# A diffusion block on one core: the residual's scaling moved in VectorE's queue, the decays' sums made float32r

## The chip, the cores and the metric

One core of a Trainium2 chip runs the whole program. The metric is the device time of an execution in microseconds (us). The engines are TensorE (PE, its weight loads PEld), VectorE (DVE), ScalarE (ACT), GpSimd (POOL) and SyncE (SP, which issues most of the DMAs).

## The reference

Two layers of a diffusion block work on 512 tokens x and 256 context tokens, 1024 wide, in float32. Each layer is a gated feed-forward, a mixer of four kinds of attention, and a second feed-forward; each is followed by a layer norm of the scaled residual plus the branch.

```python
def post_norm(x, f, g, b):
    return layer_norm(ALPHA * x + f, g, b)

def swiglu(h, w_in, w_out):
    a, u = jnp.split(h @ w_in, 2, axis=-1)
    return (jax.nn.silu(a) * u) @ w_out

def ssd_chunked(x, dt, A, Bh, Ch, h0):
    ...
    cum = jnp.cumsum(dtc * A, axis=2)
    seg = cum[:, :, :, None, :] - cum[:, :, None, :, :]
    lmat = jnp.exp(jnp.where(tril, seg, -jnp.inf))
    att = jnp.einsum('bcihn,bcjhn->bcijh', Cc, Bc) * lmat * dtc[:, :, None]
    ...
    y = y + jnp.einsum('bcihn,bchpn,bcih->bcihp', Cc, jnp.moveaxis(h_start, 0, 1), jnp.exp(cum))
```

One of the four parts of the mixer is this state-space part (SSD): in chunks of 128 tokens, 4 heads, in two directions. `seg` are sums of `dt * A` over the tokens between two, `cum` sums up to one; the second layer leaves out the context's outputs.

## The kernel before

The code is written as straight program text, and a scheduler puts each instruction into the queue of its engine; each engine works its queue in order. Some places call `tc.issue_after(ins)`: what is written inside it is queued behind `ins` on the engine of `ins`.

**Products.** A float32 matrix is split into a high part (float32r, by ACT, L328) and the rest (by DVE, L329), and a product is three float32r matmuls (`mm3`, L335 to L337).

**Feed-forward (`ffn`).** The 22 column blocks f of the hidden width are done in parts: (0,4), (4,8), ... with the context, and (0,6), (6,12), ... in the last feed-forward. In the first part, f = 0 and 1 are plain products (`first`), while DVE and POOL make sums for the others (`sums`: L573 to L576, split at L565, L566). The others are `winograd`: seven products of 12 matmuls each. In the order of the code they are B11, B21, T2, B22, T3, T4 and T1. DVE adds them up at L689 to L703; L692 reads T2 and must be done before T3 is written, since both lie in one PSUM tile, and L693 stands likewise between B22 and T4. In the last feed-forward, even f are `eight` (plain). `store` then splits the gated g (ACT L646, DVE L647). `branch_out` multiplies a part with the second weights and adds it to the residual `res` (L472, L474).

**The residual.** `res` must be scaled by ALPHA (and the norm's gain and shift, `rescale`, L465: 2 x 12 DVE operations with the context, 2 x 8 without) before the first part is added to it. This was written behind the first part as `self.behind`, and the scheduler was free to queue it earlier. For the first feed-forward it is `scale_input` (L359, 6 operations). `merge`, behind the mixer, does it too.

**SSD.** `ssd` runs beside the projections of the other attention kinds (`side_by_side`), so that their `mm3` stand between its steps in PE's queue. `chunk_out(t)` is called for 6 chunks in layer 0 (two of them in one direction) and 4 in layer 1. POOL makes `ld` = dtA times a triangle (L1294, two operations), PE sums it against another triangle (L1299, 8 float32 matmuls, which the trace holds as 16), ACT takes the exponential (L1301), DVE makes `att` (L1310 to L1313), and PE multiplies (L1319). PE also makes the decays `two` from dtA (L1330, 8 float32 matmuls, 16 in the trace; half in a one-direction chunk) and the states' part (L1332).

## Time and profile before

| what | us |
|---|---|
| median of 3 runs | 2965.39 (2965.01 to 2967.98) |
| the profiled execution | 2970.67 |
| its span | 2968.9 |

The profile is of one execution. A stretch of the span is given as start and end in us from the span's start. The feed-forwards' first parts lie at 48 to 98 (first, layer 0), 1085 to 1150 (second, layer 0), 1660 to 1730 (first, layer 1) and 2590 to 2632 (second, layer 1); the SSD chunks at 712 to 800 and 2305 to 2362. Idle time of PE is a stretch's length less its busy time; the granted clock is a share of 2.4 GHz, and a mean over the stretch of the two levels 2.4 and 1.2 GHz.

### The profile page before, as it was taken

The page shows a single profiled execution, that of the slowest core. Times are in us where ns is not written, and L with a number is a line of the kernel's source. Part 1 is how long each engine was busy: PE and PEld are TensorE (multiplying, and loading weights), DVE is VectorE, ACT ScalarE, POOL GpSimd, SP SyncE. Part 2 cuts the span into 40 slices and gives each one's busy share as a digit, 9 for nine tenths or more (in the row PEclk, how much of TensorE's full clock was granted, in tenths as well). Part 3 has the DMA queues.
Part 4 walks back from the last instruction along what each step waited for, and adds up shares of the span by engine and source line. Part 5 has one row for each costly group of instructions (what it writes and reads, how often), then busy time and mean ns, then how long its engine had stood idle before and what let it go on. Part 6 is the DMA issues. An engine that isn't in the chain of part 4 may idle for free.

```text
span 2968.9 us, 43652 instructions
## 1 busy us (share of the span) xinstructions
PE 2867.3 (97%) x16412; PEld 2451.8 (83%) x16412; DVE 2068.6 (70%) x4258; ACT 1149.6 (39%) x2103; POOL 494.2 (17%) x372
## 2 busy tenths in 40 slices
PE   7999999999999998999999999999999999899997
PEld 4898888888787777888878789999988787788886
DVE  4766668775758787666577976766886757776558
ACT  4333233352256543322324433333344256443333
POOL 1222122100110002221211122221200110012112
PEclk9999999999999999999999999999999999999998
DMA  6443334231124223534435122212132143242332
GB/s 230 144 162 107 121 100 141 77 100 49 29 78 83 94 72 104 178 122 141 157 103 168 57 67 75 76 58 74 56 97 72 44 110 89 78 125 86 95 100 72
DMA packets 319207, 296.09 MB, mean 100 GB/s; under 512 B 16311, under 2 KB 244751, under 8 KB 318739
## 3 DMA queue, kind: packets, MB, share of 16 engines
q1 hardware_dynamic: 317939, 290.80, 31.6%
q0 software_dynamic: 1056, 2.49, 0.4%
q8 instruction: 130, 2.13, 0.3%
q14 instruction: 82, 0.67, 0.1%
HBM read 270.52 MB, written 7.39 MB: 94 GB/s over the span
## 4 chain that ended last, share of the span: by engine, by line
PE 77%; DVE 15%; issue 3%; ACT 2%; DMA 2%; POOL 0%; SPq 0%; DVEq 0%; ACTq 0%; POOLq 0%
PE ps L335 12%; PE ps L337 12%; PE ps L336 12%; PE psp L335 9%; PE psp L337 9%; PE psp L336 9%; PE ps L260 2%; PE ps L1033 2%; DVE wl L329 2%; PE ps L1075 2%; DVE tmp L472 2%; PE psp L1091 2%; DVE res L465 2%; DVE res L474 1%; DVE actl L392 1%
## 5 line engine op out<-in xcount | busy, mean ns | idle before, releaser
L328 ACT CAST wh<-wraw 128x512 fp32r<-128x512 f32 x570 | 352.1, 621 | 873.2 <-PE ps L337 457.2
L329 DVE TENSOR_TENSOR wl<-wraw,wh 128x512 fp32r<-128x512 f32 x570 | 416.0, 736 | 330.4 <-ACT wh L328 324.2
L335 PE MATMUL psp<-acth,wh 128*128 128x384 f32 (+2 forms) x1432 | 482.9, 338 | 4.5 <-DVE e L701 1.9
L336 PE MATMUL psp<-actl,wh 128*128 128x384 f32 (+2 forms) x1432 | 481.0, 336 | 5.1 <-DVE actl L392 4.9
L337 PE MATMUL psp<-acth,wl 128*128 128x384 f32 (+2 forms) x1432 | 478.6, 335 | 4.6 <-DVE wl L329 4.6
L335 PEld LDWEIGHTS psp<-acth,wh 128*128 128x128 f32 x1432 | 271.6, 190 | 44.7 <-issue 27.3
L328 ACT CAST wh<-wrax 128x512 fp32r<-128x512 f32 x280 | 173.9, 622 | 339.9 <-PE ps L336 201.6
L336 PEld LDWEIGHTS psp<-actl,wh 128*128 128x128 f32 x1432 | 271.9, 190 | 20.3 <-DVE actl L392 7.0
L337 PEld LDWEIGHTS psp<-acth,wl 128*128 128x128 f32 x1432 | 272.2, 190 | 16.2 <-DVE wl L329 5.2
L335 PE MATMUL ps<-S,wh 128*128 128x384 f32 (+1 forms) x840 | 276.7, 329 | 7.8 <-DVE e L692 4.8
L336 PE MATMUL ps<-S,wh 128*128 128x384 f32 (+1 forms) x840 | 275.8, 328 | 0.0
L337 PE MATMUL ps<-S,wl 128*128 128x384 f32 (+1 forms) x840 | 275.6, 328 | 0.0
L329 DVE TENSOR_TENSOR wl<-wrax,wh 128x512 fp32r<-128x512 f32 x280 | 212.5, 764 | 84.3 <-ACT wh L328 59.0
L335 PE MATMUL ps<-acth,wh 128*128 128x512 f32 (+2 forms) x688 | 245.7, 358 | 3.2 <-ACT wh L328 1.7
L336 PE MATMUL ps<-actl,wh 128*128 128x512 f32 (+2 forms) x688 | 244.2, 355 | 0.0
L337 PE MATMUL ps<-acth,wl 128*128 128x512 f32 (+2 forms) x688 | 243.3, 354 | 0.0
L335 PE MATMUL ps<-wh,gTh 128*128 128x512 f32 x594 | 235.1, 396 | 7.6 <-DVE tmp L472 7.6
L337 PE MATMUL ps<-wh,gTl 128*128 128x512 f32 x594 | 233.4, 393 | 0.0
L336 PE MATMUL ps<-wl,gTh 128*128 128x512 f32 x594 | 233.4, 393 | 0.0
L474 DVE TENSOR_TENSOR res<-res,tmp 128x512 f32<-128x512 f32 x268 | 188.0, 732 | 0.6
L335 PEld LDWEIGHTS ps<-S,wh 128*128 128x128 f32 x840 | 159.2, 189 | 12.6 <-issue 6.8
L337 PEld LDWEIGHTS ps<-S,wl 128*128 128x128 f32 x840 | 159.3, 190 | 0.0
(376 smaller groups left out, 5470.8 us busy)
## 6 DMA issues: line engine op xcount, KB each, us to landing
araw<-in_ada_w_dram SPq DMA_DIRECT2D x128, 512.0 KB
wraw<-in_ffn_w_out_dram SPq DMA_DIRECT2D x88, 512.0 KB
wrax<-in_ffn_w_in_dram SPq DMA_DIRECT2D x160, 256.0 KB
wraw<-in_ffn_w_in_dram SPq DMA_DIRECT2D x120, 256.0 KB
wraw<-in_mix_w_in_dram SPq DMA_DIRECT2D x44, 512.0 KB
wraw<-in_ffn_w_in_dram SPq DMA_DIRECT2D x36, 512.0 KB
wraw<-in_mix_w_out_dram SPq DMA_DIRECT2D x16, 512.0 KB
mrow<-mrow SPq DMA_DIRECT2D x10, 512.0 KB
```

The costliest lines, as they stand in the source:

```text
L260: nc.tensor.matmul(ps[32 * g:32 * g + 32, :], lhsT=self.cs[:, k, c0:c0 + 32], rhs=w[:, k - kk, :], start=i == 0 and k < 4, stop=i == len(n ...
L328: self.nc.scalar.copy(h, raw)
L329: self.nc.vector.tensor_tensor(lo, raw, h.bitcast(F32), op=ALU.subtract)
L335: mm(out, lhsT=a[0], rhs=b[0], start=start, stop=False)
L336: mm(out, lhsT=a[0], rhs=b[1], start=False, stop=False)
L337: return mm(out, lhsT=a[1], rhs=b[0], start=False, stop=stop)
L465: nc.vector.tensor_tensor(r, r, x[:, lo:hi], op=op)
L472: nc.vector.tensor_tensor(y, acc, mrow[0 if t < 4 else 1][:, dh * 512:(dh + 1) * 512], op=ALU.mult)
L474: nc.vector.tensor_tensor(r, r, y, op=ALU.add)
L1033: nc.tensor.matmul(ps[:, at:at + hi - lo], lhsT=q, rhs=part[:, lo:hi], start=i == 0, stop=i == 1)
L1075: nc.tensor.transpose(pt[:, j * P:(j + 1) * P], p[:, a:a + P], self.ident)
L1091: nc.tensor.matmul(out[64 * a:64 * a + 64, :], lhsT=v[:, kt, vcol:vcol + 64], rhs=pT[:, i], start=i == 0, stop=i == len(order) - 1)
```

## The change

Two things. First, `rescale` and `scale_input` get a step, and `ffn` calls them at the last two f of the first part: one half is queued behind the store of the last but one f, the other behind that of the last. The loads and ACT's work on the gain come before the step and are not bound. Second, in `ssd`, dtA is split into two float32r parts. `ld` becomes four tiles: the high parts by POOL, the low ones by ACT (8 operations a chunk), as products with U and L. PE sums them with GT and LT as weights, in 4 matmuls of 512 columns for all heads. `two` is made from the same `ld` tiles, with two weights `half` that hold ones in 64 columns, in 8 matmuls of 256 columns. So `ld`, which has one buffer, is now read until `two` is done.

```diff
--- before.py
+++ after.py
@@ -355,6 +355,7 @@
             self.nc.sync.dma_start(self.res[i], src)
 
     def scale_input(self, pool, tiles):
+        yield
         for r in self.res:
             self.nc.vector.tensor_scalar(r, r, ALPHA, None, op0=ALU.mult)
             yield
@@ -458,6 +459,7 @@
         gb = self.gain(l, i, self.side or tmp, tags)
         for x in gb:
             nc.scalar.mul(x, x, ALPHA)
+        yield
         for lo, hi in ((0, 512), (512, D)):
             for t in tiles:
                 for x, op in zip(gb, (ALU.mult, ALU.add)):
@@ -644,7 +646,7 @@
         def store(g, f, lo):
             gh, gl = gT[0][:, f - lo], gT[1][:, f - lo]
             nc.scalar.copy(gh, g)
-            nc.vector.tensor_tensor(gl, g, gh.bitcast(F32), op=ALU.subtract)
+            return nc.vector.tensor_tensor(gl, g, gh.bitcast(F32), op=ALU.subtract)
 
         def first(late):
 
@@ -722,10 +724,17 @@
                     winograd(f, g, todo[1:])
                 else:
                     eight(f, g)
-                store(g, f, lo)
+                end = store(g, f, lo)
+                if lo == 0 and f >= hi - 2:
+                    if f == hi - 2:
+                        behind = self.behind(pool, tiles)
+                        next(behind)
+                    with self.tc.issue_after(end.ins):
+                        next(behind)
             if lo == 0:
-                for _ in self.behind(pool, tiles):
-                    pass
+                with self.tc.issue_after(end.ins):
+                    for _ in behind:
+                        pass
             if mrow is None:
                 mrow = self.mod_rows(l, which, pool, (0, 1) if with_ctx else (0,))
             a_of = lambda f, t: tuple(g[:, f - lo, t * P:(t + 1) * P] for g in gT)
@@ -1218,6 +1227,18 @@
         self.softplus(dtf, tmp)
         dtA = self.sb(tmp, [6, 8], "dtA")
         nc.vector.tensor_tensor(dtA, dt, bcast1(self.A[:, l], 6), op=ALU.mult)
+
+        parts = [self.sb(tmp, [6, 8], x, F32R) for x in ("dtAh", "dtAl")]
+        nc.scalar.copy(parts[0], dtA)
+        nc.vector.tensor_tensor(parts[1], dtA, parts[0].bitcast(F32), op=ALU.subtract)
+        before = [self.sb(tmp, [P], x, F32R) for x in ("GTr", "LTr")]
+        for x, m in zip(before, (GT, LT)):
+            nc.scalar.copy(x, m)
+
+        halves = [self.sb(tmp, [P], f"half{a}", F32R) for a in range(2)]
+        for a, x in enumerate(halves):
+            nc.vector.tensor_copy(x, self.zero.to_broadcast([P, P]))
+            nc.vector.tensor_copy(x[:, 64 * a:64 * a + 64], self.ones[:, :64])
         ps = self.ps1()
         for d, m in ((0, GT), (1, LT)):
             nc.tensor.matmul(ps[:, 24 * d:24 * d + 24].rearrange("p (t e) -> p t e", t=6), lhsT=m,
@@ -1288,15 +1309,18 @@
             q = col(t)
             first = {4: (1,), 5: (0,)}.get(t, (0, 1))
 
+            seg = self.ps1()
             ld = []
-            for d, m in ((0, GT), (1, LT)):
-                x = self.sb(tmp, [4, P], f"ld{d}", bufs=1)
-                nc.gpsimd.tensor_tensor(x, bcast(dtA[:, t, 4 * d:4 * d + 4], P), bcast1(m, 4), op=ALU.mult)
-                ld.append(x)
-            seg = self.ps1()
-            for h in range(4):
-                for d, m in ((0, U), (1, L)):
-                    nc.tensor.matmul(seg[:, h * P:(h + 1) * P], lhsT=ld[d][:, h], rhs=m, start=d == 0, stop=d == 1)
+            for d, m in ((0, U), (1, L)):
+                hi, lo = (self.sb(tmp, [4, P], f"ld{d}{i}", F32R, bufs=1) for i in range(2))
+                ld.append((hi, lo))
+                nc.gpsimd.tensor_tensor(hi, bcast(parts[0][:, t, 4 * d:4 * d + 4].bitcast(F32), P), bcast1(m, 4),
+                                        op=ALU.mult)
+                for h in range(4):
+                    nc.scalar.mul(lo[:, h], m, parts[1][:, t, 4 * d + h:4 * d + h + 1].bitcast(F32))
+                for i, x in enumerate((hi, lo)):
+                    nc.tensor.matmul(seg, lhsT=before[d], rhs=x.rearrange("p h c -> p (h c)"), start=d + i == 0,
+                                     stop=d + i == 2)
             E = self.sb(tmp, [2, 2, P], "segE", bufs=1)
             nc.scalar.activation(E.rearrange("p g r c -> p (g r c)"), seg, AF.Exp)
             G = self.ps1()
@@ -1320,15 +1344,14 @@
                                          rhs=att[d][:, pr, a], start=d == 0, stop=d == 1)
 
             two = self.ps2()
-            for d, m in ((0, U), (1, L)):
-                if d not in first:
-                    continue
+            for d in first:
+                for i in range(4):
+                    x = ld[d][i // 2].rearrange("p (r a) c -> p a r c", a=2)[:, i % 2]
+                    nc.tensor.matmul(two[:, 0, 256 * d:256 * d + 256].rearrange("p (r c) -> p r c", r=2), lhsT=halves[i % 2],
+                                     rhs=x, start=i == 0, stop=i == 3)
+            for d in first:
                 for pr in range(2):
                     at = (2 * d + pr) * P
-                    for a in range(2):
-                        e = 4 * d + 2 * pr + a
-                        nc.tensor.matmul(two[64 * a:64 * a + 64, 0, at:at + P],
-                                         lhsT=dtA[:, t, e:e + 1].to_broadcast([P, 64]), rhs=m, start=True, stop=True)
                     nc.tensor.matmul(two[:, 1, at:at + P], lhsT=state[t][:, d, pr * P:(pr + 1) * P],
                                      rhs=uT[:, 4 + pr, q:q + P], start=True, stop=True)
             lo, hi = 256 * first[0], 256 * first[-1] + 256
```

The scheduler's order of the changed program differs at these places (line numbers of the changed program are larger: L403 to L405 for L402 to L404, L467 for L465, L649 for L647, L691 to L705 for L689 to L703, L1322 for L1299, L1350 for L1330).

VectorE, second feed-forward of layer 0, while the last residual tiles are normalized (`rs` is the reciprocal root, `mrow` the gain and shift). Before:

```order
L402 TENSOR_TENSOR rs_2092_10454<-rs_2091_10453 128x2
L465 TENSOR_TENSOR res_1983_9845<-res_1983_9845,mrow_2202_11131 128x512
L403 SCALAR_TENSOR_TENSOR rs_2092_10454<-rs_2092_10454,rs_2090_10452 128x2
L465 TENSOR_TENSOR res_1984_9846<-res_1984_9846,mrow_2202_11131 128x512
L404 SCALAR_TENSOR_TENSOR rs_2091_10453<-rs_2092_10454,rs_2091_10453 128x2
L465 TENSOR_TENSOR res_1983_9845<-res_1983_9845,mrow_2203_11132 128x512
L402 TENSOR_TENSOR rs_2092_10454<-rs_2091_10453 128x2
L465 TENSOR_TENSOR res_1984_9846<-res_1984_9846,mrow_2203_11132 128x512
L403 SCALAR_TENSOR_TENSOR rs_2092_10454<-rs_2092_10454,rs_2090_10452 128x2
L465 TENSOR_TENSOR res_1985_9847<-res_1985_9847,mrow_2202_11131 128x512
L404 SCALAR_TENSOR_TENSOR rs_2091_10453<-rs_2092_10454,rs_2091_10453 128x2
```

Of the change, the same place and on to the split of the context's turned input (`acth`, `actl`):

```order
L405 SCALAR_TENSOR_TENSOR rs_2109_10503<-rs_2110_10504,rs_2109_10503 128x2
L403 TENSOR_TENSOR rs_2110_10504<-rs_2109_10503 128x2
L404 SCALAR_TENSOR_TENSOR rs_2110_10504<-rs_2110_10504,rs_2108_10502 128x2
L405 SCALAR_TENSOR_TENSOR rs_2109_10503<-rs_2110_10504,rs_2109_10503 128x2
L437 SCALAR_TENSOR_TENSOR bnm_10517<-bnmv_10413,rs_2109_10503 128x2
L392 CAST acth_64<-S_2015_9953 128x256
L576 TENSOR_TENSOR e_2144_10758<-S_2015_9953 128x384
L393 TENSOR_TENSOR actl_65<-S_2015_9953,acth_64 128x256
```

The rescaling of `res` is gone from between the steps of `rs`; before, 15 of its 24 rows stood between the rows of the last norms, 7 more ahead of the store of f = 2, and 2 behind it.

VectorE, same feed-forward, the end of f = 2 and the begin of f = 3 (`gTl` is the store, `psp` and `ps` hold f = 3's products). Before:

```order
L329 TENSOR_TENSOR wl_11017<-wrax_10988,wh_11016 128x512
L329 TENSOR_TENSOR wl_11022<-wrax_10988,wh_11021 128x512
L647 TENSOR_TENSOR gTl_10520<-ffg_10841,gTh_10519 128x768
L465 TENSOR_TENSOR res_1988_9850<-res_1988_9850,mrow_2202_11131 128x512
L689 TENSOR_TENSOR ffg_10986<-psp_11042,e_2194_11025 128x384
L465 TENSOR_TENSOR res_1988_9850<-res_1988_9850,mrow_2203_11132 128x512
L329 TENSOR_TENSOR wl_11172<-wraw_11169,wh_11171 128x512
L692 TENSOR_TENSOR e_2196_11040<-ps_2199_11057,e_2194_11025 128x384
L329 TENSOR_TENSOR wl_11176<-wraw_11169,wh_11175 128x512
L693 TENSOR_TENSOR e_2197_11041<-ps_2200_11058,e_2196_11040 128x384
```

Of the change, from the end of the 12 rows that stand behind that store:

```order
L467 TENSOR_TENSOR res_2006_9900<-res_2006_9900,mrow_2195_11036 128x512
L467 TENSOR_TENSOR res_2005_9899<-res_2005_9899,mrow_2196_11037 128x512
L467 TENSOR_TENSOR res_2006_9900<-res_2006_9900,mrow_2196_11037 128x512
L691 TENSOR_TENSOR ffg_11054<-psp_11110,e_2214_11093 128x384
L694 TENSOR_TENSOR e_2216_11108<-ps_2219_11125,e_2214_11093 128x384
L329 TENSOR_TENSOR wl_11222<-wraw_11219,wh_11221 128x512
L695 TENSOR_TENSOR e_2217_11109<-ps_2220_11126,e_2216_11108 128x384
L329 TENSOR_TENSOR wl_11226<-wraw_11219,wh_11225 128x512
L702 TENSOR_TENSOR e_2217_11109<-psp_11180,e_2217_11109 128x384
```

All 12 rows of a half now stand between the store of f = 2 and the first add of f = 3, and 12 more behind the store of f = 3. All seven weight splits of f = 3 stand ahead of the first 12.

TensorE of the changed program, same feed-forward, f = 3: T1 (`psp_11180`) has moved ahead of T3 (`ps_2219`, second half).

```order
L335 MATMUL psp_11180<-acth_64,wh_11089 128x384
L336 MATMUL psp_11180<-actl_65,wh_11089 128x384
L337 MATMUL psp_11180<-acth_64,wl_11090 128x384
L335 MATMUL psp_11215<-wh_11221,gTh_10569 128x512
L335 MATMUL ps_2219_11125<-S_2147_10765,wh_11079 128x384
L336 MATMUL ps_2219_11125<-S_2148_10766,wh_11079 128x384
```

The row between them opens the second weights' product in the PSUM tile that L691 has to read first, and T3 waits for L694. So five products of f = 3, and not four, stand ahead of the first wait for VectorE.

TensorE, SSD of layer 0, `two` of the third token chunk and what follows. Before (`two` of that chunk and the next `att` product):

```order
L1330 MATMUL ps_1292_7185<-cst_5376,dtA_6030 64x128 x2
L1332 MATMUL ps_1292_7185<-uT_5397,st_1001_5393 128x128
L1330 MATMUL ps_1292_7185<-cst_5376,dtA_6030 64x128 x2
L1332 MATMUL ps_1292_7185<-uT_5397,st_1001_5393 128x128
L1330 MATMUL ps_1292_7185<-cst_5376,dtA_6030 64x128 x2
L1332 MATMUL ps_1292_7185<-uT_5397,st_1001_5393 128x128
L1330 MATMUL ps_1292_7185<-cst_5376,dtA_6030 64x128 x2
L1332 MATMUL ps_1292_7185<-uT_5397,st_1001_5393 128x128
L1319 MATMUL ps_1304_7237<-att_1300_7225,xw_7226 64x128 x2
L1319 MATMUL ps_1304_7237<-segE_7220,xw_7226 64x128 x2
L1319 MATMUL ps_1304_7237<-att_1300_7225,xw_7226 64x128 x2
L1319 MATMUL ps_1304_7237<-segE_7220,xw_7226 64x128 x2
```

Of the change, from the last rows of `two` to the next chunk's sums:

```order
L1350 MATMUL ps_1308_7229<-ld_1299_7194,half_1080_6040 128x256
L1350 MATMUL ps_1308_7229<-ld_1299_7194,half_1081_6041 128x256
L1350 MATMUL ps_1308_7229<-ld_1300_7195,half_1080_6040 128x256
L1350 MATMUL ps_1308_7229<-ld_1300_7195,half_1081_6041 128x256
L1355 MATMUL ps_1308_7229<-uT_5397,st_1001_5393 128x128 x4
L1322 MATMUL ps_1311_7251<-ld_1312_7252,GTr_6036 128x512
L1322 MATMUL ps_1311_7251<-ld_1313_7253,GTr_6036 128x512
L1322 MATMUL ps_1311_7251<-ld_1314_7261,LTr_6037 128x512
L799 MATMUL ps_1287_7146<-ident_90,tB_7168 128x128 x2
L1322 MATMUL ps_1311_7251<-ld_1315_7262,LTr_6037 128x512
```

Before, the sums of the last chunk stood some 15 rows ahead of this `two`. Now they follow it at once, and have to wait until POOL and ACT have filled `ld` again.

## Rows read from the trace of the kernel before

**Rows 1.** The page, part 1: busy time, share of the span, instructions of each engine.

```profile
PE 2867.3 (97%) x16412; PEld 2451.8 (83%) x16412; DVE 2068.6 (70%) x4258; ACT 1149.6 (39%) x2103; POOL 494.2 (17%) x372
```

**Rows 2.** Windows: stretch, its length, busy time of each engine, granted clock, DMA.

```profile
48.00:98.00 50.00, 46.22 (x288) 40.25 (x291) 49.21 (x86) 31.52 (x61) 21.06 (x12) 1.00 0.38 126
1085.00:1150.00 65.00, 56.93 (x315) 50.83 (x315) 63.18 (x117) 34.41 (x64) 19.13 (x12) 0.97 0.22 66
1660.00:1730.00 70.00, 62.67 (x340) 55.80 (x340) 68.14 (x126) 37.33 (x69) 17.86 (x12) 0.95 0.23 69
2590.00:2632.00 42.00, 37.58 (x252) 34.55 (x252) 41.26 (x80) 23.49 (x53) 10.03 (x7) 0.96 0.38 110
712.00:800.00 88.00, 83.44 (x531) 65.96 (x529) 61.35 (x169) 18.89 (x34) 14.11 (x13) 0.94 0.12 34
2305.00:2362.00 57.00, 53.70 (x361) 44.02 (x359) 40.87 (x108) 14.89 (x26) 9.60 (x11) 1.00 0.18 50
```

**Rows 3.** Waits of PE, 1085 to 1150: total us, times, longest.

```profile
PE psp L337 <- DVE wl L329: 2.2, 1, 2.2
...
PE ps L335 <- DVE e L692: 1.8, 1, 1.8
```

**Rows 4.** Timeline, DVE, 1095 to 1150: start, us, instruction, shapes, count.

```profile
1096.50 3.08 DVE L465 TENSOR_TENSOR res<-res,mrow 128x512 f32<-128x512 f32 x5
...
1145.43 0.55 DVE L700 TENSOR_TENSOR e<-psp,e 128x384 f32<-128x384 f32 x1
...
1148.58 0.95 DVE L647 TENSOR_TENSOR gTl<-ffg,gTh 128x768 fp32r<-128x768 f32 x1
```

**Rows 5.** Timeline, DVE, 2590 to 2632.

```profile
2614.55 4.68 DVE L465 TENSOR_TENSOR res<-res,mrow 128x512 f32<-128x512 f32 x4
...
2620.36 5.39 DVE L465 TENSOR_TENSOR res<-res,mrow 128x512 f32<-128x512 f32 x7
...
2626.88 0.68 DVE L642 TENSOR_TENSOR ffg<-ps,ffg 128x512 f32<-128x512 f32 x1
```

**Rows 6.** Waits of PE, 2590 to 2632.

```profile
PE ps L335 <- DVE ffg L642: 2.9, 1, 2.9
```

**Rows 7.** Timeline, PE, 712 to 756.

```profile
714.69 0.39 PE L335 MATMUL psp<-acth,wh 128*128 128x512 f32 x1
...
714.92 0.39 PE L336 MATMUL psp<-actl,wh 128*128 128x512 f32 x1
...
736.62 0.44 PE L1330 MATMUL ps<-cst,dtA 128*64 128x128 f32 x4
...
736.99 0.49 PE L1332 MATMUL ps<-uT,st 128*128 128x128 f32 x2
...
749.26 1.95 PE L1299 MATMUL ps<-cst,ld 128*128 128x128 f32 x16
...
751.04 0.61 PE L1304 MATMUL ps<-uT 128*128 128x128 f32 x4
```

**Rows 8.** Timeline, POOL and DVE, 750 to 754.

```profile
751.13 2.04 POOL L1294 TENSOR_TENSOR ld<-dtA,cst 128x512 f32<-128x512 f32 x2 [12.93 <-PE ps L1299]
...
751.27 0.92 DVE L402 TENSOR_TENSOR rs<-rs 128x8 f32<-128x8 f32 x1
...
752.23 0.97 DVE L403 SCALAR_TENSOR_TENSOR rs<-rs,rs 128x8 f32<-128x8 f32 x1
...
753.23 0.17 DVE L404 SCALAR_TENSOR_TENSOR rs<-rs,rs 128x8 f32<-128x8 f32 x1
```

**Rows 9.** Waits of PE: first 712 to 800, then 2305 to 2362.

```profile
PE ps L1319 <- DVE att L1312: 4.5, 3, 1.7
...
PE ps L1319 <- DVE att L1312: 2.2, 2, 1.5
```

**Rows 10.** Groups of ACT by line and shape: busy us, mean ns, idle before.

```profile
L1099 ACT COPY oT<-psp 128x128 f32<-128x128 f32 x40 | 10.6, 265 | 15.8 <-PE psp L1091 15.2
```

## The prediction

> **What bounds the kernel now.** The page's first part comes first: PE is busy in 2867.3 us, 97% of the span, DVE in 70%, ACT in 39%, POOL in 17% [rows 1]. So a gain must either take matmul time away, or remove idle time of PE and the lower clock that comes with it. There are some 100 us of idle time in all, and the next question is where the change can reach any.
>
> The windows answer it [rows 2]; their columns are the length, then PE, PEld, DVE, ACT, POOL, clock. In the four first parts of the feed-forwards, DVE is the full engine: 49.21 of 50 us, 63.18 of 65, 68.14 of 70, 41.26 of 42. PE idles there 3.78, 8.07, 7.33 and 4.42 us, 23.6 in all. The granted clock was 1.00, 0.97, 0.95 and 0.96, a mean of stretches at 2.4 GHz and some at 1.2; (1 - clock) x length gives what this costs, 0, 1.95, 3.5 and 1.7, or 7.15 us. Together 30.75 us lie in the places from which the change takes work off DVE.
>
> The waits confirm the engine: PE waits 2.2 us for a weight split of DVE (L329) and 1.8 for L692 [rows 3], and in the last feed-forward 2.9 us for the add L642 [rows 6]. DVE's timeline says what those stood behind: five L465 in one piece [rows 4], and in the last feed-forward 4 and 7 of them directly before that L642, which begins at 2626.88 [rows 5]. No later work needs the scaled residual before the first part's second product.
>
> In SSD the picture is another: DVE is busy in 61.35 of 88 us, PE idles 4.56 and lost 0.06 x 88 = 5.3 us to the clock in layer 0; in layer 1, 3.30 us and none [rows 2]. PE's named wait is that of L1319 for `att` (L1312): 4.5 us in three, 2.2 in two [rows 9].
>
> **Part A, the scaling moved.** One L465 costs 3.08 / 5 = 0.62 us, 0.60 from start to start [rows 4]. A feed-forward with context loses 24 of them (14.4 us) from the stretch where DVE is full, the last one 16 (9.6 us); 22 of the 24 stood ahead of f = 2's store. That is more than PE's idle time in each of these stretches. Not all of it comes back: after DVE, PE waits for the splits of ACT and for what POOL sums. The bounds are 0 and the whole 30.75; I take two thirds, since each named long wait stands behind DVE and the rest of the idle time is in pieces that no view puts down to one engine: **-20.5**.
>
> The 12 instructions of a half now stand in one piece. The first piece is the one that can hurt. From the start of L700, when PE has gone on to f = 3, to the end of f = 2's store took 1145.43 to 1149.53, 4.1 us [rows 4]. Then 12 x 0.60 = 7.2 us, so L691 and L694 are through about 12 us after PE began f = 3. All weight splits of f = 3 stand ahead of the piece, and PE has five products before it needs L694. A matmul of 512 columns takes 0.23 us from start to start [rows 7], one of 384 columns 0.17, a product of 12 then 2.05, five 10.3. PE waits 12 - 10.3 = 1.6 us in two feed-forwards. In the last one a piece is 8 x 0.60 = 4.8 us, f = 4 (`eight`) ends with one add of 0.68 [rows 5], a split and a store, some 2.3 in all, and the two first adds of f = 5 need 0.7; five products with 256 columns cover 6.9 of these 7.8: 0.9. Together **+4.1**; the bounds are 0, if DVE now runs ahead by more than this, and 10, if PE has only four products' cover. The stretches with up to 3.78 us idle kept the clock at 1.00 and those from 4.42 did not [rows 2]; a third of 8.07 plus 1.6 is 4.3, between the two. So I give back half of the two thirds counted of (1.95 + 3.5): **+1.8**. The second piece stands behind the store of f = 3; what follows on PE is the first half of `branch_out`, 6 tiles x 12 matmuls x 0.23 = 16.5 us, whose weights are split ahead of the piece: nothing, and some 5 us if that cover were missing. The load of the gain now waits for the scaling in the last feed-forward, but is first needed after these products: nothing. `scale_input` (6 operations, in the first stretch) has its share in the two thirds. A is -20.5 + 4.1 + 1.8 = **-14.6**.
>
> **Part B, the decays.** PE's timeline gives both old prices. The 16 records of L1299 last from 749.26 to 751.04, when L1304 starts: 1.78 us [rows 7]. Four L1330 take 736.62 to 736.99, 0.37, so 16 take 1.48 [rows 7]. The new forms aren't in the trace: float32r with 512 columns is priced by L335 at 0.23 (714.69 to 714.92), with 256 columns by half of it. `seg` becomes 4 x 0.23 = 0.92, 0.86 less, in ten chunks **-8.6**. `two` becomes 8 x 0.115 = 0.92, 0.56 less in eight chunks and 0.28 in the two with one direction, **-5.0**. If 256 columns cost as much as 512, `two` would be 1.84 and the term +3.2; I take the half, because 128-column records come at less than half of 0.23 already [rows 7].
>
> `ld` had to wait for the sums alone, so POOL refilled it right behind them: 2.04 us from 751.13. Meanwhile two tiny operations of DVE, 0.17 us elsewhere, took 0.92 and 0.97, ahead of `gm` and `att`: 1.55 us on the chain that PE then awaits for up to 1.7 [rows 8, 9]. Now POOL waits for `two`, after which this chain is through in the middle chunks. I take -1.5 for each of two chunks, **-3.0** (bounds 0 and all 6.7 us of that wait), and half of SSD's clock loss, **-2.65** (bounds 0 and 5.3).
>
> This is where the Trainium skill has a rule: SBUF — State Buffer, section "Who interferes with whom", says that a VectorE instruction with two SBUF inputs and a GpSimd instruction that reads SBUF shut each other out for a whole instruction. The trace agrees, with 0.92 and 0.97 for 0.17 [rows 8]. The rule speaks against part A as well, since each L465 has two inputs there: see the fourth rival.
>
> On the other side: in the first chunks of layer 1 the shorter fill leaves PE waiting for `att`, **+1.0** (bounds 0 and the 1.7 saved there). In the last chunk of each layer the sums now stand directly behind the previous `two`. They need POOL's two operations (1.02 each [rows 8]) and ACT's eight, 0.265 each by the nearest 128x128 copy [rows 10], 2.1 together; the two run side by side, and PE can start on the first direction at about half. With the signals between them I take 0.9 us each, **+1.8** (bounds 0 and 6, both in full and behind other ACT work). In the other chunks some 40 matmuls of other attention kinds, 40 x 0.23 = 9 us, stand between `two` and the next sums. ACT gets 80 operations, 21 us, but is busy in 18.89 of 88 there [rows 2]. The set-up (8 small operations a layer) has the projections to hide behind: nothing, or 2 us without them. B is -8.6 - 5.0 - 3.0 - 2.65 + 1.0 + 1.8 = **-16.5**.
>
> **Sum.** -14.6 - 16.5 = -31. The profiled execution took 2970.67, 5.3 above the median of the runs, so it would be some 2939.6; the median 2965.4 becomes 2934.4. Forecast **2935**.
>
> **Rivals.** A measurement of this kernel tells a change from none at about 0.2%, 5.9 us.
>
> 1. DVE isn't all that holds the first parts: ACT (37.33 of 70 us [rows 2]) or POOL's sums end the wait as soon as DVE is done, and one third comes back. A is -10.3 + 5.9 = -4.4, the whole -21: 2944. For it: POOL and DVE alternate there, with waits no view adds up. Against: DVE is 98% full.
>
> 2. In SSD PE comes sooner to L1319 and waits for `att` instead, since the chain from `seg` over ACT and DVE stays as long. Half of the 13.6 us is lost, and neither the stretch nor the clock comes back: B is -6.8 + 2.8 = -4, the whole -19: 2947. For it: that wait exists already [rows 9]. Against: 9 us of other matmuls in most chunks.
>
> 3. Slower. With one buffer, `ld` is read till `two`, and the refill (2.04 by POOL, 2.1 by ACT behind its other work) becomes the wait in all ten chunks instead of two. If 2.1 us are open, and the clock falls with it as in layer 0 (5.3 lost at 4.56 idle [rows 2]), a chunk costs 2.1 + 2.4 = 4.5 us: B is -13.6 + 45 = +31, and with A +17: 2982. It decides from (14.6 + 13.6) / 10 = 2.8 us a chunk. Against: the 9 us of cover.
>
> 4. The pieces of 12 meet POOL. L465 took 4.68 / 4 = 1.17 us in [rows 5], and 12 of those take 14 us: 6.8 us more of a wait in two feed-forwards, 4.6 in the last, 18 in all, so A is about +4, the whole -13: 2952. The skill's rule above gives the mechanism. Against: POOL's work was 19.13 of 65 us, and 17.86 of 70 [rows 2], and it makes sums for f = 2 and 3 that must be done before these products.
>
> 5. No difference: 2 and 4 together, or the gains of A given back in the part behind.
>
> That the scaling doesn't move at all is excluded by the order of VectorE's queue.
>
> **How the numbers follow.** The forecast has 0.55 (its own range 2924 to 2941), rival 1 has 0.17, 2 has 0.11, 4 has 0.05, 5 has 0.06, 3 has 0.06. Faster is the forecast with 1, 2 and 4: 0.88; the same 0.06; slower 0.06. The range goes down to 2919 (all of the 30.75 and the whole SSD clock returned: -46) and up to 2955, which takes in rivals 1, 2 and 4.
>
> **What would show it.** Right: no L467 between the norms; DVE no longer full before f = 2, PE idle in these four windows down to some 12 us with the clock near 1.00; a new wait of PE for L691 or L694 of 1 to 2 us behind the piece; L1322 four times at 0.23 and L1350 eight times at 0.115; the `rs` operations behind `seg` at 0.17; one PE wait of about 1 us for `ld` in each layer's last chunk. Wrong: PE's idle time in the first parts as before, under names of ACT or POOL; L467 at over 1 us; L1350 at 0.23; waits of L1322 for `ld` in every chunk.

## The result, and the profile after

| kernel | median us | runs | ratio to before | 95% interval |
|---|---|---|---|---|
| before | 2966.26 | 4 | | |
| changed | 2948.06 (2945.49 to 2950.82) | 4 | 0.9938 | 0.9921 to 0.9956 |

The change makes the kernel 18.2 us (0.6%) faster. The forecast was 2935, 31 us faster; the time lies in its range, but four tenths of the gain are missing. The profiled execution has a span of 2946.7 us. The page's first part, which answers to [rows 1]:

```profile
PE 2844.7 (97%) x16220; PEld 2437.1 (83%) x16220; DVE 2071.0 (70%) x4268; ACT 1171.5 (40%) x2189; POOL 497.3 (17%) x372
```

PE is busy 22.6 us less in a span that is 22.2 us shorter: PE idles as long as before, 102 us. So idle time that was taken away in one place came back in another. To find the places, both kernels are cut at the same instructions of PE. First before, in three stretches that begin ahead of the last three feed-forwards' first parts and go on into the part behind, then the two SSD stretches (columns as in [rows 2]):

```profile
1074.00:1189.00 115.00, 103.53 (x541) 89.69 (x540) 95.51 (x171) 53.42 (x93) 25.02 (x16) 0.99 0.28 87
1650.00:1789.00 139.00, 131.13 (x676) 115.40 (x675) 117.51 (x216) 59.63 (x104) 30.77 (x21) 0.98 0.22 66
2564.00:2709.00 145.00, 135.71 (x789) 119.38 (x788) 106.71 (x218) 65.84 (x125) 23.51 (x17) 0.96 0.34 103
712.00:830.00 118.00, 112.53 (x727) 89.05 (x726) 79.66 (x221) 27.25 (x50) 15.42 (x15) 0.96 0.17 46
2290.00:2385.00 95.00, 91.70 (x588) 74.60 (x587) 64.18 (x170) 26.10 (x46) 10.08 (x11) 1.00 0.23 60
```

The same windows of the changed kernel, and under them the four first parts alone, which answer to the first four of [rows 2]:

```profile
1066.70:1176.20 109.50, 101.20 (x540) 87.51 (x539) 93.16 (x171) 52.83 (x93) 27.08 (x16) 1.00 0.30 92
1636.50:1773.70 137.20, 130.07 (x676) 114.85 (x675) 118.77 (x216) 58.70 (x104) 32.82 (x21) 0.98 0.22 66
2544.90:2687.00 142.10, 134.47 (x789) 118.88 (x788) 104.14 (x218) 65.60 (x125) 22.18 (x16) 0.98 0.35 105
711.46:825.47 114.01, 103.25 (x615) 83.91 (x614) 80.77 (x222) 38.08 (x90) 15.95 (x15) 0.96 0.18 50
2274.71:2365.69 90.98, 85.53 (x508) 70.04 (x507) 65.22 (x170) 33.21 (x70) 10.23 (x11) 1.00 0.23 63
...
47.90:97.40 49.50, 47.53 (x289) 41.44 (x292) 44.83 (x80) 31.05 (x60) 19.16 (x12) 0.97 0.37 122
1077.60:1136.20 58.60, 54.62 (x316) 48.85 (x315) 47.72 (x95) 33.59 (x64) 18.33 (x12) 1.00 0.25 74
1647.00:1710.90 63.90, 59.66 (x340) 53.91 (x341) 56.12 (x106) 36.03 (x68) 15.96 (x12) 0.97 0.25 77
2571.70:2607.20 35.50, 35.50 (x252) 33.19 (x251) 30.23 (x64) 23.34 (x53) 8.12 (x8) 1.00 0.41 118
```

The four first parts alone went as forecast: DVE is no longer full (47.72 of 58.6 us), and PE's idle time, length less busy, is 1.97, 3.98, 4.24 and 0, 10.2 us instead of 23.6. But over the three longer stretches only 10.2 us were won (399.0 to 388.8), so some of it is lost again right behind. In SSD it is the reverse of what was hoped: PE is busy 15.5 us less (204.23 to 188.78), and idles 10.76 + 5.45 = 16.2 us instead of 5.47 + 3.30 = 8.8. Of 15.5 us only 8.0 remain (213.0 to 205.0). The stretches that were edited are 10.2 + 8.0 us shorter, which comes to the 18.2 of the medians.

The waits name both losses. Those of PE in the changed kernel, in the order of the first five windows above:

```profile
PE psp L335 <- DVE ffg L691: 2.1, 1, 2.1
...
PE ps L335 <- DVE tmp L474: 1.0, 1, 1.0
...
PE psp L335 <- DVE ffg L691: 1.8, 1, 1.8
...
PE ps L335 <- DVE tmp L474: 0.7, 1, 0.7
...
PE psp L335 <- DVE tmp L474: 1.8, 1, 1.8
PE psp L335 <- DVE ffg L691: 1.5, 1, 1.5
...
PE ps L799 <- DVE tB L896: 3.6, 2, 1.8
PE psp L335 <- DVE dqT L915: 2.4, 1, 2.4
PE psp L792 <- DVE pcol L837: 1.4, 1, 1.4
PE ps L1343 <- DVE segE L1336: 1.4, 1, 1.4
PE ps L1343 <- DVE att L1336: 0.7, 2, 0.5
...
PE ps L1343 <- DVE att L1336: 1.9, 3, 1.2
PE ps L799 <- DVE tB L896: 1.3, 1, 1.3
```

Behind the first parts stands the forecast new wait, for the first add behind the piece of scalings: 5.4 us in three feed-forwards. In SSD, the wait for `att` has fallen from 6.7 [rows 9] to 2.6 us, and PE now waits for names that were not on the list, `tB`, 4.9 us, `pcol` and `segE`, and longer for `dqT` (0.9 us before). VectorE's timeline shows the piece, 12 scalings in 7.30 us, and the add behind it:

```profile
1134.56 0.94 DVE L649 TENSOR_TENSOR gTl<-ffg,gTh 128x768 fp32r<-128x768 f32 x1
1135.43 7.30 DVE L467 TENSOR_TENSOR res<-res,mrow 128x512 f32<-128x512 f32 x12
1142.65 0.54 DVE L691 TENSOR_TENSOR ffg<-psp,e 128x384 f32<-128x384 f32 x1
...
758.70 0.97 DVE L404 SCALAR_TENSOR_TENSOR rs<-rs,rs 128x4 f32<-128x4 f32 x1
759.70 0.97 DVE L405 SCALAR_TENSOR_TENSOR rs<-rs,rs 128x4 f32<-128x4 f32 x1
```

The second half of that fence is SSD. Two steps of the reciprocal root `rs`, which another attention kind needs for its `tB`, take 0.97 us each; the next one, at 760.70, takes 0.17. Just then GpSimd refills `ld`, as its timeline shows:

```profile
758.61 2.04 POOL L1317 TENSOR_TENSOR ld<-dtAh,cst 128x512 fp32r<-128x512 f32 x2 [22.54 <-PE ps L1350]
```

It was released by `two` (L1350), as forecast. PE's timeline has the wait that follows (in brackets: idle time and what ended it), and the new matmuls' prices, from start to start: 1.01 us for `seg` (718.08 to 719.09, forecast 0.92) and 1.04 for a full `two` (2294.15 to 2295.19, forecast 0.92).

```profile
718.08 0.70 PE L1322 MATMUL ps<-ld,GTr 128*128 128x512 f32 x2
...
719.09 0.61 PE L1328 MATMUL ps<-uT 128*128 128x128 f32 x4
...
762.83 0.44 PE L799 MATMUL ps<-ident,tB 128*128 128x128 f32 x2 [1.82 <-DVE tB L896]
...
2294.15 1.20 PE L1350 MATMUL ps<-ld,half 128*128 128x256 f32 x8
2295.19 0.61 PE L1355 MATMUL ps<-uT,st 128*128 128x128 f32 x4
```

### The profile page after: what moved, and what is told of

Read it like the earlier page. It is cut to its first block, busy times and chain, and to the rows that moved or that the text cites. A ratio compares the mean times of both kernels' runs of the same rounds, so it can differ in the third digit from the quotient of the medians.

```text
span 2946.7 us, 43367 instructions
## 1 busy us (share of the span) xinstructions
PE 2844.7 (97%) x16220; PEld 2437.1 (83%) x16220; DVE 2071.0 (70%) x4268; ACT 1171.5 (40%) x2189; POOL 497.3 (17%) x372
## 4 chain that ended last, share of the span: by engine, by line
PE 81%; DVE 12%; issue 3%; ACT 2%; DMA 1%; POOL 0%; SPq 0%; DVEq 0%; ACTq 0%; POOLq 0%
PE ps L335 13%; PE ps L337 13%; PE ps L336 13%; PE psp L335 10%; PE psp L337 10%; PE psp L336 10%; PE ps L260 2%; PE ps L1042 2%; PE ps L1084 2%; DVE tmp L474 2%; PE psp L1100 2%; DVE res L476 2%; DVE wl L329 1%; DVE res L467 1%; DVE actl L393 1%
## 5 line engine op out<-in xcount | busy, mean ns | idle before, releaser
L336 PEld LDWEIGHTS psp<-actl,wh 128*128 128x128 f32 x1432 | 271.3, 189 | 14.6 <-issue 2.6
L476 DVE TENSOR_TENSOR res<-res,tmp 128x512 f32<-128x512 f32 x268 | 189.1, 736 | 0.6
```

The lines of the kernel that those rows point to most:

```text
L336: mm(out, lhsT=a[0], rhs=b[1], start=False, stop=False)
L476: nc.vector.tensor_tensor(r, r, y, op=ALU.add)
```

## The experiments

Theory: the two parts add up; what is missing is the wait behind the piece of 12 in the one, and GpSimd's refill, which stretches the next chain of `rs` behind `two`, in the other. Rivals: the waits come from elsewhere (the shift of the stage, ScalarE's extra work, the shorter matmuls as such), or VectorE's work comes back at another wait however it is cut. The times of all kernels:

| kernel | median us | before, same chip | ratio | 95% interval |
|---|---|---|---|---|
| scaling moved alone | 2955.12 | 2966.51 | 0.9960 | 0.9948 to 0.9972 |
| decays alone | 2959.23 | 2966.51 | 0.9977 | 0.9969 to 0.9986 |
| no scaling | 2933.96 | 2966.51 | 0.9889 | 0.9877 to 0.9902 |
| high parts by ScalarE | 2936.37 | 2966.51 | 0.9896 | 0.9884 to 0.9909 |
| piece cut in two | 2935.35 | 2965.96 | 0.9889 | 0.9871 to 0.9906 |
| old `two` | 2943.83 | 2965.96 | 0.9919 | 0.9906 to 0.9932 |
| high parts by ScalarE, `ld` twice | 2933.56 | 2965.96 | 0.9888 | 0.9873 to 0.9902 |
| cut, and high parts by ScalarE | 2922.69 | 2965.96 | 0.9851 | 0.9836 to 0.9866 |
| all scalings behind the last f | 2942.55 | 2967.57 | 0.9915 | 0.9902 to 0.9929 |
| high parts by VectorE | 2934.09 | 2967.57 | 0.9888 | 0.9874 to 0.9901 |
| cut, ScalarE, `ld` twice | 2923.45 | 2967.57 | 0.9849 | 0.9836 to 0.9862 |

**The scaling alone, the decays alone.** Each is one half of the change's diff; of the first:

```diff
-                store(g, f, lo)
+                end = store(g, f, lo)
+                if lo == 0 and f >= hi - 2:
+                    if f == hi - 2:
+                        behind = self.behind(pool, tiles)
+                        next(behind)
+                    with self.tc.issue_after(end.ins):
+                        next(behind)
```

and of the second:

```diff
+                for i, x in enumerate((hi, lo)):
+                    nc.tensor.matmul(seg, lhsT=before[d], rhs=x.rearrange("p h c -> p (h c)"), start=d + i == 0,
+                                     stop=d + i == 2)
```

> The scaling is moved as in the change, SSD is that of before. Theory 1 (the parts are independent, and each gives what the two traces show stage by stage): -7 us of idle time in the four first parts and some -2 us by the clock, so 8 to 10 us less than before; the new wait of PE for the first add behind the piece of 12 (ffg, 1.5 to 2.1 us) is there in three feed-forwards. Theory 2 (the move gives nothing by itself, the gain of the whole change is SSD's): within 3 us of before.

> SSD's decays are made as in the change, the scaling stands as before. Theory 1: 14 us less matmul time, 7 to 8 us of it returned as waits in SSD (of PE's transposes for tB and tC, and in the last chunk), so 6 to 10 us less than before, more only where the clock falls less often. Theory 2 (the waits in SSD come from the other part, which shifted the stage): the waits of SSD as before (4.6 and 3.3 us of idle time), 13 to 16 us less.

Measured: 11.4 and 7.3 us less, together 18.7, the whole change 18.2; theory 1 had given the first 8 to 10 and the second 6 to 10. The parts add up, and each shows its own losses: with the decays alone PE is busy 102.30 of 113.08 and 85.54 of 91.00 us in the two SSD stretches, so it idles 10.8 and 5.5 us there without the scaling having moved. Theory 2 of that run falls: the waits are the decays' own.

**No scaling.** How much of the first parts' time is the scaling's at all?

```diff
                 for x, op in zip(gb, (ALU.mult, ALU.add)):
                     r = self.res[t][:, lo:hi]
-                    nc.vector.tensor_tensor(r, r, x[:, lo:hi], op=op)
+                    if tags[0] != "mrow0" or self.in_merge:
+                        nc.vector.tensor_tensor(r, r, x[:, lo:hi], op=op)
```

> The changed kernel without the 24, 24 and 16 scaling operations of the last three feed-forwards: the residual isn't scaled there, so this part of the computation is left out. Theory 1 (the rest of the idle time in the first parts belongs to VectorE's other work, and only the piece of 12 is the scaling's): the wait for ffg is gone (2.1 + 1.8 + 1.5 us), nothing else, 4 to 6 us less than the changed kernel. Theory 2 (the scaling still holds the first parts): PE's idle time there falls to some 4 us in all, 12 us or more less than the changed kernel.

14.1 us less than the changed kernel. Both theories were off: the wait for `ffg` is gone as theory 1 said, but 14 us are more than its 4 to 6; and theory 2's 4 us of idle time are not reached: in the four first parts, cut at the same places, PE still idles 10.4 us without any scaling, as in the changed kernel. The windows of the longer stretches, which answer to the first three of the changed kernel:

```profile
1066.30:1172.90 106.60, 100.87 (x541) 87.52 (x540) 79.36 (x147) 53.12 (x93) 23.81 (x17) 1.00 0.25 75
1632.10:1763.30 131.20, 126.54 (x676) 111.74 (x675) 104.93 (x192) 59.12 (x104) 28.73 (x21) 1.00 0.23 69
2534.00:2673.00 139.00, 134.27 (x790) 118.83 (x789) 96.87 (x202) 66.20 (x125) 21.11 (x16) 0.98 0.35 103
```

Length less busy gives 5.7, 4.7 and 4.7 us of idle time, 15.1, against 23.1 in the changed kernel: 8 us, of which `ffg` is 5.4 and most of the rest shorter waits for `tmp` (L474). In the second stretch the clock is 1.00 instead of 0.98. The 15 us that stay are not the scaling's.

**The piece cut in two.** 6 scalings behind the store of f = 2, 6 in the middle of f = 3, the rest (12, or 8) as in the changed kernel. The add that the second 6 stand behind is that of B22; the expectation calls it the add that frees T2's tile, which is the one before it.

```diff
-            for t in tiles:
+            for half in (tiles[:len(tiles) // 2], tiles[len(tiles) // 2:]):
...
+                yield
...
-            add(c12, product(two[:, 0], w["B22"], "S4"), u)
+            end = add(c12, product(two[:, 0], w["B22"], "S4"), u)
+            if part is not None:
+                with self.tc.issue_after(end.ins):
+                    next(part)
```

> The changed kernel with the first piece cut in two: 6 scalings (4 in the last feed-forward) behind the store of the last but one f, 6 in the middle of the last f, behind the add that frees the tile of T2. Theory 1 (the wait for ffg is the length of the piece less its cover): 3.6 us less in front of that add, more than the 1.5 to 2.1 us waited, so the three waits for ffg are gone, and the time is 4 to 6 us less than the changed kernel's. Theory 2 (what is taken from this wait comes back at the next add, since VectorE has the same work to do before the second product's tiles are free): within 2 us of the changed kernel.

12.7 us less than the changed kernel, twice what was expected. Its windows:

```profile
1067.10:1174.00 106.90, 101.16 (x541) 87.58 (x541) 90.92 (x169) 51.37 (x91) 20.20 (x14) 1.00 0.32 94
1633.60:1764.90 131.30, 126.61 (x676) 111.63 (x675) 116.60 (x214) 58.38 (x104) 29.75 (x21) 1.00 0.23 69
2537.60:2677.50 139.90, 135.13 (x789) 118.97 (x788) 103.38 (x218) 65.64 (x125) 21.77 (x17) 0.98 0.36 106
```

These are the lengths of the kernel without scaling to 1.3 us in 377. The 64 scalings cost nothing any more: idle time is 15.2 us, as without them. PE waits 0.3 and 1.2 us for the second add of f = 3 in the two feed-forwards with context, and for `tmp` 0.2 at most instead of 1.0, 0.7 and 1.8. So theory 1 was right about the wait and too small, since the waits for `tmp` went too (their causes are below, under the second piece), and the clock in the second stretch went to 1.00. Of the 12.7 us, 10.7 lie in these stretches.

**All behind the last f.** The other way to get rid of the first piece:

```diff
-                    with self.tc.issue_after(end.ins):
-                        next(behind)
```

> The changed kernel with all scalings (24, 24, 16) behind the store of the last f, none behind that of the last but one. Theory 1 (PE's wait is what a piece exceeds its cover by, and the cover of branch_out's first half is 16.5 us): the waits for ffg (2.1, 1.8, 1.5 us) are gone; the piece of 14.6 us leaves the first add of the second half 6 to 7 us later than now, some 5 us of it as a wait in each of the two feed-forwards with context and 3 in the last: 3 to 10 us more than the changed kernel. Theory 2 (the second weights' cover is enough): 5 to 8 us less than the changed kernel, as with the piece cut in two.

5.5 us less, which is theory 2's time. Its reason isn't there, though. PE's waits (the first of the next two) and VectorE's timeline (the second), second feed-forward of layer 0:

```profile
PE psp L335 <- DVE tmp L474: 2.2, 1, 2.2
```

```profile
1146.55 14.53 DVE L467 TENSOR_TENSOR res<-res,mrow 128x512 f32<-128x512 f32 x24
```

The piece of 14.5 us overhangs its cover by 2.2 us, in place of the 2.1 for `ffg`: a wait moved, not removed, in the two feed-forwards with context. In the three stretches this kernel takes 388.5 us, the changed one 388.8; idle time fell by 2.3 in the last one and changed by less than 1 us in the others. Theory 1's wait is real but half as long as it said, and the 5.5 us lie mostly outside what was edited: 3.1 of them in layer 0's SSD stretch (110.9 us instead of 114.0), whose program is the same, with the clock at 0.98 instead of 0.96. Why it fell less often there stays open.

**Who makes `tB` late: the high parts by ScalarE, and by VectorE.** GpSimd's operation is taken out in two ways. By ScalarE:

```diff
-                nc.gpsimd.tensor_tensor(hi, bcast(parts[0][:, t, 4 * d:4 * d + 4].bitcast(F32), P), bcast1(m, 4),
-                                        op=ALU.mult)
                 for h in range(4):
+                    nc.scalar.mul(hi[:, h], m, parts[0][:, t, 4 * d + h:4 * d + h + 1].bitcast(F32))
```

> The changed kernel with the high parts of ld made by ScalarE too (8 more small operations a chunk, none by GpSimd). Theory 1 (GpSimd's refill behind two stretches the rs chain on VectorE, and PE's transposes wait for its tB): the rs operations last 0.17 us instead of 0.9 to 1.0, the waits for tB (1.8, 1.8 and 1.3 us) fall by 1.5 us each, and the time by 3 to 5 us, less 2 us or so in the last chunks, where ScalarE now needs twice the time to fill ld. Theory 2 (tB is late for another reason): the same waits for tB, and 0 to 5 us more than the changed kernel.

By VectorE:

```diff
-                nc.gpsimd.tensor_tensor(hi, bcast(parts[0][:, t, 4 * d:4 * d + 4].bitcast(F32), P), bcast1(m, 4),
+                nc.vector.tensor_tensor(hi, bcast(parts[0][:, t, 4 * d:4 * d + 4].bitcast(F32), P), bcast1(m, 4),
```

> The changed kernel with the high parts of ld by VectorE, two operations of some 0.6 us a chunk, none by GpSimd; in the queue they stand between the rs steps. Theory 1 (GpSimd's sharing of the port with the rs steps is what makes tB late, not ScalarE's extra work, which is as in the changed kernel): 1.2 us of own work take the place of 1.6 us of lengthening, no rs step lasts over 0.3 us, the waits for tB are 0.3 to 0.8 us shorter each, and the time is 0 to 5 us less. Theory 2 (ScalarE's eight operations in front of ec are what delays the chain): the waits for tB as in the changed kernel, time 3 us more.

11.7 and 14.0 us less than the changed kernel, far more than theory 1 allowed, in its direction. With ScalarE, VectorE's same two steps at the same place, then PE's transpose and SSD's windows:

```profile
757.49 0.16 DVE L404 SCALAR_TENSOR_TENSOR rs<-rs,rs 128x4 f32<-128x4 f32 x1
757.68 0.16 DVE L405 SCALAR_TENSOR_TENSOR rs<-rs,rs 128x4 f32<-128x4 f32 x1
```

```profile
760.00 0.44 PE L799 MATMUL ps<-ident,tB 128*128 128x128 f32 x2 [0.20 <-DVE tB L896]
```

```profile
711.44:817.71 106.27, 101.22 (x615) 82.09 (x614) 73.71 (x222) 49.75 (x130) 4.43 (x5) 0.97 0.20 53
2265.16:2352.63 87.47, 85.17 (x508) 69.95 (x507) 61.19 (x170) 40.17 (x94) 3.82 (x5) 1.00 0.24 65
```

0.97 became 0.16, the wait of 1.82 became 0.20, and both stretches together take 193.7 us: 11.3 less than in the changed kernel, 19.3 less than before, with 7.4 us of idle time instead of 16.2. So nearly all of the 11.7 us lie here; with VectorE the two stretches take 194.1 us. `att`, `pcol` and `segE` are off the list too; with VectorE, where `segE` still costs 0.8 us, `pcol` is gone as well. That ScalarE got 80 more operations changed none of this, and in the run with VectorE, where ScalarE does what it does in the changed kernel, the steps are short as well, though the two operations of `ld` stand between them (here the one ahead of L404):

```profile
757.28 0.68 DVE L1317 TENSOR_TENSOR ld<-dtAh,cst 128x512 fp32r<-128x512 f32 x1
757.88 0.15 DVE L404 SCALAR_TENSOR_TENSOR rs<-rs,rs 128x4 f32<-128x4 f32 x1
```

ScalarE as the cause is out; it is GpSimd beside VectorE.

**The old `two`.** `ld` is free behind the sums again:

```diff
-                for i in range(4):
-                    x = ld[d][i // 2].rearrange("p (r a) c -> p a r c", a=2)[:, i % 2]
...
+                    for a in range(2):
+                        e = 4 * d + 2 * pr + a
+                        nc.tensor.matmul(two[64 * a:64 * a + 64, 0, at:at + P],
+                                         lhsT=dtA[:, t, e:e + 1].to_broadcast([P, 64]), rhs=(U, L)[d], start=True, stop=True)
```

> The changed kernel with the old two (float32 from dtA), so that ld is free right behind the sums: part of the second edit alone. Theory 1 (what SSD waits is made by the place of GpSimd's refill): the rs operations behind the sums last 0.9 again and the wait is again for att (some 4.5 and 2.2 us), the waits for tB are gone, the last chunk has its cover back (no waits for segE, dqT as before 0.9); 5 us more matmul time than the changed kernel, about 6 us less waiting: within 3 us of it. Theory 2 (the waits come from the shorter matmuls as such): waits between those of before and of the changed kernel, 2 to 5 us more than the changed kernel.

4.2 us less than the changed kernel, but only 0.8 of it lies in the SSD stretches (204.2 us instead of 205.0): PE is busy 7.1 us more there (195.87 instead of 188.78) and idles 7.9 less (8.4 instead of 16.2). So the new `two`, which saves matmul time, gains nothing in that kernel as it stands; the other 3.4 us lie outside the edit. GpSimd's timeline and VectorE's:

```profile
747.96 2.19 POOL L1317 TENSOR_TENSOR ld<-dtAh,cst 128x512 fp32r<-128x512 f32 x2 [12.45 <-PE ps L1322]
```

```profile
749.21 0.97 DVE L400 TENSOR_SCALAR rs<-rs 128x8 int32<-128x8 int32 x1
```

The lengthening (L400 takes 0.17 in the changed kernel) went along with GpSimd, back ahead of `gm`, and PE waits for `att` again (2.0 and 0.5 us, less than the 4.5 and 2.2 expected); for `tB` it still waits 0.8; for `dqT` it waits 3.8, which theory 1 had wrong.

**Two buffers for half of `ld`,** on top of the high parts by ScalarE:

```diff
-                hi, lo = (self.sb(tmp, [4, P], f"ld{d}{i}", F32R, bufs=1) for i in range(2))
+                hi, lo = (self.sb(tmp, [4, P], f"ld{d}{i}", F32R, bufs=2 - d) for i in range(2))
```

> The changed kernel with the high parts by ScalarE, and two buffers for the first direction's ld. Theory 1 (what is left in the last chunk is the wait for ld, 1.1 us, and the shorter chain behind it): half of ld is ready before, so this wait falls to 0.5 us or less and the wait for dqT (2.4 us) shrinks by the same, 1 to 2 us less than the kernel with the high parts by ScalarE alone. Theory 2 (the last chunk's end is a chain of ScalarE and VectorE from the sums on): no difference within 1 us.

2933.56 against 2936.37, within the two intervals of one another; in SSD's first stretch the wait of 1.1 us for `ld` is gone, but one of 1.5 us for `ec` is there instead and `dqT` stays at 2.4. PE's idle time in that stretch is 5.0 us with and without the buffer, so it is theory 2 by the waits, though the median is 2.8 us lower: the last chunk's end is a chain.

**Together.** The cut piece with the high parts by ScalarE, then with the second buffer too:

> Both: the first piece cut in two, and the high parts by ScalarE. Theory 1 (they add up): 4 to 6 us less than the kernel with the high parts by ScalarE alone, near 2931. Theory 2 (the cut gives nothing): 2936, as that kernel.

> The cut piece, the high parts by ScalarE, and two buffers for the first direction's ld. Theory 1 (the three add up): 1 to 3 us less than without the second buffer, some 2920. Theory 2 (the last chunk's end is a chain behind the sums that the buffer doesn't shorten): within 1 us of 2922.7.

2922.69 and 2923.45: the first two add up, to 25.4 us below the changed kernel and 43.3 below before, more than theory 1's 4 to 6 us for the cut, as with the cut alone; the mean clock was 0.994, in the changed kernel 0.990. The second buffer gives nothing.

## Why the prediction was right or wrong

**What bounds it.** Right: the first parts were VectorE's, and their idle time fell by 13.4 us, with 3.7 us of the clock's 7.15 (0.97 of 49.5 us and of 63.9 still leave 3.4). "Two thirds", 20.5 us, came out as 17.1. The kernel without scaling shows that the rest belongs to other work. The order that the prediction read off the stretches (1.00 with up to 3.78 us idle, less from 4.42 on) did not hold: the first stretch now has 0.97 with 1.97 us idle.

**The first piece.** Right in mechanism, 5.4 us instead of 4.1: the place is the first add, L691, and not L694, because a product of the second weights needs L691's tile and stands ahead of T3 in PE's queue. Cutting the piece removed it.

**The second piece at nothing.** Right for the piece itself. The 16.5 us of cover are shorter in fact (14.5 us of scalings already overhung by 2.2), but still longer than 7.3. The waits for `tmp` behind it, 1.0, 0.7 and 1.8 us, have other causes that the prediction did not price. VectorE's timeline in the second feed-forward of layer 0, then GpSimd's, then VectorE's in the last feed-forward:

```profile
1165.41 2.87 DVE L476 TENSOR_TENSOR res<-res,tmp 128x512 f32<-128x512 f32 x2
...
1166.10 1.62 POOL L611 TENSOR_TENSOR wraw<-wraw 128x512 f32<-128x512 f32 x1
...
2650.33 0.69 DVE L329 TENSOR_TENSOR wl<-wraw,wh 128x512 fp32r<-128x512 f32 x1 [2.06 <-ACT wh L328]
```

Two adds (L476) in front of the awaited L474 took 2.87 us, 1.28 at 1163.01, while GpSimd worked on weights (L610 from 1164.73, then L611); in layer 1 the same two took 2.54 beside GpSimd, for a wait of 0.7. In the last feed-forward VectorE stood 2.06 us at a weight split whose high part ScalarE had yet to make, ahead of the awaited L474. In the kernel with the cut piece the second piece is as long, GpSimd came to its L611 only at 1173.30, and these waits were 0.2 us at most; whether they go by the cut or by the shift of the stage was not tried. The clock's share was taken as +1.8; the second stretch, at 0.98 before and after, gave nothing back. In all, part A was -11.4 instead of -14.6.

**The matmuls.** Right in size, 15.5 us less busy time in SSD, 13.6 forecast, but by two misses that partly cancel. `seg` and `two` cost 0.09 and 0.12 us a chunk more than forecast. The states' products, which were left out, got cheaper now that they no longer stand between the pieces of `two`: 9.8 us of busy time before (L1332) and 5.8 after (L1355) in layer 0, 7.8 and 5.0 in layer 1.

**The chain behind `seg`.** This is the step that failed: "Now POOL waits for `two`, after which this chain is through in the middle chunks", priced -3.0 with -2.65 for the clock. The chain to `att` did become short, and its waits fell by 4.1 us. But GpSimd's 2.04 us lie now on the next chain of `rs`, that of `tB`, which PE's transposes need at once: 4.9 us for `tB`, 1.4 for `pcol`, and no clock won back (0.96 before and after). The prediction asked what the refill leaves, not what it moves onto. Taking GpSimd out made the SSD stretches 19.3 us shorter than before, more than the 16.5 forecast for part B, whose own time was 7.3.

**The last chunk.** +1.8 for `ld`: this wait is not on the list of the changed kernel. What came is the uncovered chain from its sums on, `segE` 1.4 and `dqT` 2.4 instead of 0.9 us. Part of it (`segE`) went with GpSimd, the end at `dqT` did not.

**The rivals.** The forecast's own range, 2924 to 2941, was missed; the time lies in the stated one because that takes in the rivals. The second came true in size (2947 against 2948.06), with the wait at another name than `att` and part A less than forecast too, so that its number fits by luck. The rule of the Trainium skill (SBUF — State Buffer, "Who interferes with whom") was weighed against the scaling and left in the fourth rival; it should have been asked of every place to which the refill could move. The scalings themselves weren't touched: 7.30 / 12 = 0.61 us each. The third, `ld` open in every chunk, did not come. What is not settled: how much of the medians is the clock. It falls in places that nothing was edited in, too: its mean was 0.93 at 929 to 979 us before (3.5 us lost) and 1.00 at 922 to 970 in the changed kernel. So the two profiled executions differ by 22.2 us, 4 more than the medians and the edited stretches, and 2 to 4 us between two single executions can be the clock alone.

## What to carry to other kernels

When a buffer is released later, look up what its refill will run beside from then on: an engine that nobody waits for can still lengthen one that is waited for. Work that is to fill another engine's slack should be cut to pieces shorter than the cover at each place; 12 in one piece cost 5.4 us; with 6 and 6 PE idled no longer than without any scaling. Saved matmul time counts only if the chain that feeds the next wait gets shorter with it: the new `two` saved 7.1 us and gave back 7.9.

## What the runs showed of the hardware

VectorE's steps with a single input were held up too: an int32 tensor_scalar (L400) took 0.97 us beside GpSimd, 0.17 in most other places. And the other way round: while VectorE ran its 12 scalings in 7.31 us, none of them lengthened, one operation of GpSimd took 5.38 us, where 65 of the 70 of its line took 1.27 to 1.84; the one beside the twelve of 1135.43 took 4.54. VectorE's twelve began at 1709.73; GpSimd's timeline, changed kernel, layer 1:

```profile
1712.79 5.38 POOL L610 TENSOR_TENSOR wrax<-wrax,wrax 128x512 f32<-128x512 f32 x1 [9.54 <-DMA wrax<-in_ffn_w_in_dram]
```

The Trainium skill (SBUF — State Buffer, section "Who interferes with whom") says that the one that issues later is blocked. Here GpSimd began later and lost, for several instructions on end; in [rows 5] it was VectorE that lost, with 1.17 us for 0.60.
